# Layer 1 of a two-layer decoder trunk: the first group's scores are put three product steps earlier

## The chip, the cores and the metric

The kernel runs on one core of one Trainium2 chip. The metric is the device time of one execution in microseconds, as the median of several runs. The engines are named as in the profile: PE (TensorE matmul), PEld (its weight loads), DVE (VectorE), ACT (ScalarE), POOL (GpSimd), SP (SyncE, which issues the weight transfers). A code such as L439 is line 439 of the kernel before.

## The reference, cut to what matters

One sequence of 256 tokens, width 1024, two layers, 16 heads of 64. Layer 0 has an attention of its own with q, k and v. Layer 1 projects only q; its k and v have 4 heads and come from the residual stream in front of it. Each layer ends with a gated feed-forward with a causal convolution of width 3.

```python
hk = rmsnorm(x, kv_norm)
k, v = jnp.split(hk @ w_kv_b, 2, axis=-1)
shared_k = to_bhsd(partial_rope(heads(k, N_KV_HEADS), cos, sin))
shared_v = to_bhsd(heads(v, N_KV_HEADS))
...
h = rmsnorm(x, attn_norm[l])
q = partial_rope(heads(h @ w_q_b[i], N_HEADS), cos, sin)
o = swa_sink_attention(to_bhsd(q), shared_k, shared_v, sinks_b[i])   # window 128, a sink per head
x = x + o.transpose(0, 2, 1, 3).reshape(B_, S_, N_HEADS * HEAD_DIM) @ w_o
x = x + conv_ffn(rmsnorm(x, ffn_norm[l]), w_up[l], conv_w[l], conv_b[l], w_down[l])
```

## The kernel before, in words

All matrices are float32. Each operand of a large product is split into a high part (rounded to the matmul's format) and a low part (the rest), and a product is three matmuls: high by high, high by low, low by high. Weights come in units of 128 x 2048. SP transfers a unit (L170), ACT makes its high part (L181), DVE its low part (L189, or L191 with a gain), POOL the low part of a few (L187). Four units have room at a time.

The 256 tokens are two blocks of 128, b = 0 and 1. In layer 1, `q_half(a)` projects eight heads of q: for each block 8 steps of three products of 512 columns (L345 to L347, a "query step"), then `rotate`: ACT copies the result (L1013), DVE applies the rotary (L374 to L380, "the rope"), PE transposes (L386), ACT makes the high part of the transposes (L397) and DVE the low part (L392). The first half, `q_half(0)`, is run in full; the second is filler for the attention.

`attention` goes over four groups of four heads. `scores(g)` first issues six products of block 0 (L432 to L434), then twelve of block 1 (L439), which need the high and low parts of both blocks. Then the softmax: DVE adds the mask and takes the extreme (L457), ACT the exponential (L468), POOL merges (L463), DVE and ACT normalise (L473, L480, L478). `probs_T` transposes a pair of heads (L493), and ACT and DVE copy it out (L502, L499). `values(g)` is sixteen products with v (L538), copied out by ACT (L545, high) and DVE (L546, low). The filler after the second query half is the output projection, `Down.units(0, 3)`: units 0, 1 and 2 of it, each in four steps of six products (L587, L588, L590), called U1 to U12 in order of issue. Unit k needs the output of group k. Unit 3 and the additions to the residual (`finish`) come after the attention, and then the feed-forward (products L680 to L682).

The order of issue is written by a planner in the Python code. It has a clock of its own in nanoseconds that each piece of PE work advances by `tick`. Work for the other engines is put off with `chain(key, (wait, step), ...)`: a step is issued at the first tick at or past its due time, and the next step's wait counts from there. `require(key)` issues at once what is left under a key. A query step ticks 640 (L345 to L347), a step of the projection 1280. `fill(ns)` adds to a budget and takes filler steps until it is at or below zero; the rest is carried on:

```python
ready(oT)
fill(lead)
manual.close()
n_g = NH // 4
state = scores(0)
for g in range(n_g):
    pT = []
    for p in range(2):
        fill(rate(g)[p])
        pT.append(probs_T(2 * g + p, state[p]))
    fill(rate(g)[2])
    if g + 1 < n_g:
        state = scores(g + 1)
    ...
    values(g, pT)
```

From the attention of layer 0 on, the issued order is a priority: the program is scheduled so that an engine whose next instruction is not ready in the scheduler's reckoning takes a later one that is. On the chip each engine then runs its list in order.

Of the kernel before, what the change touches and what calls it, by code (L numbers as in the profile page):

```python
# [61 lines left out]
def trunk(ctx: ExitStack, tc, x, xw, pos, cpk, fin, w, out):  # L62
# [20 lines left out]
    def quad(dt=F32R, name="q"):  # L83
        return spaced(qd, 4 * S, dt, "q", nm(name), 15).rearrange("p (c t) -> p c t", c=4)
# [9 lines left out]
    def bank(tag):  # L94
        return ps.tile([P, 512], F32, tag=tag, name=nm(tag), bufs=4 if tag == "acc" else 2)
# [241 lines left out]
    def proj(o, hT, b, wv, units=()):  # L337

        n = o.shape[-1]
        o = pairs(o)  # L340
        for c in range(KC):
            require("x", b, c // 4)
            xh, xl = hx(hT, c)
            wh, wl = (turns(t) for t in wv(c))
            nc.tensor.matmul(o, xh[:, blk(b)], wh, start=(c == 0), stop=False)  # L345
            nc.tensor.matmul(o, xh[:, blk(b)], wl, start=False, stop=False)  # L346
            nc.tensor.matmul(o, xl[:, blk(b)], wh, start=False, stop=(c == KC - 1))  # L347
            tick(3 * n / 2.4)
            if units and (c + 1) * len(units) % KC == 0:
                used(units[(c + 1) * len(units) // KC - 1])  # L350
            yield 3 * n / 2.4

    def cols512(u):
        def wv(c):
            need(u + c // 4)
            hi, lo = wq[u + c // 4]
            s_ = slice((c % 4) * 512, (c % 4 + 1) * 512)
            return hi[:, s_], lo[:, s_]
        return wv
# [39 lines left out]
    def rotate(o, n, b, hi, lo, key, copy, then=None, wait=750.0, turn=1000.0):  # L399

        t = mid()[:, :n * P]
        chain(key, (150.0, lambda: copy(t)),
              (wait, lambda: rope(t.rearrange("p (h d) -> p h d", d=HD), 2 * n, b)),
              (turn, lambda: to_feature(t, n, b, hi, lo, key, then)))
# [499 lines left out]
    def diagonal(g):  # L904
        return lambda p: (kd[g % 2][:, p, 0], kd[g % 2][:, p, 1])

    mask = one.tile([P, S], F32, name="mask")
# [11 lines left out]
    qk = {}  # L919
# [89 lines left out]
    qk = {}  # L1009

    def q_out(t, b, o):
        require("rs", b)
        nc.scalar.activation(t, o, AF.Copy, scale=rs1[b])  # L1013

    def q_half(a):
        hi, lo = quad(), quad()
        u = U_QB + 2 * a
        for b in range(NB):
            o = bank("acc")
            yield from proj(o, xT, b, cols512(u), (u, u + 1) if b else ())  # L1020
            rotate(o, 4, b, hi, lo, ("qk", 2 * a), lambda t, b=b, o=o: q_out(t, b, o),
                   turn=2500.0 if a else 1000.0)
        for g in (2 * a, 2 * a + 1):
            c = slice(2 * (g % 2), 2 * (g % 2) + 2)
            qk[g] = (hi[:, c], lo[:, c], kT[:, 0:2], kT[:, 2:4], lambda p, a=a: a, lambda p, a=a: diagonal(0)(a))

    run(q_half(0))
    o_down = []

    def filler_b():  # L1030
        yield from q_half(1)
        yield from o_down[0].units(0, 3)
# [1 line left out]
    def ready_b(oT):  # L1034
        o_down.append(Down(U_OB, 4, oT, lambda i: require("o", i)))

    attention(qk, ready_b, filler_b(), 2800.0, lambda g: (2700.0, 1400.0, 1000.0) if g else (3300.0, 1700.0, 1000.0), mask, lambda h: 2 * (h // 8) + h % 2, True)

    hT = new_hT()
    y = [quad(F32, "y") for _ in range(2)]  # L1040
# [151 lines left out]
```

## Time and profile before

| | |
|---|---|
| median of 3 runs | 548.95 us (548.45 to 549.39) |
| the profiled execution | 548.46 us, span 546.7 us |
| busy, share of the span | PE 98%, weight loads 90%, DVE 76%, ACT 68%, POOL 24% |
| granted TensorE clock | 0.998 |
| the second query half to the feed-forward's first product | 311.24 to 364.78 us |
| first transposes of the half's last block, first scores L432, L439 | 314.48, 314.83, 316.54 us |

Times in a timeline are microseconds from the start of the span: start, length, engine, line, operation, output and inputs, shapes, and how many instructions of the kind follow each other; square brackets hold idle time of the engine in front of it and what ended that. The rows of PE overlap, since a product's end is modelled with its way through the array; the step from start to start is what it takes. In the table of waits stand who waited for whom, the sum in us, how often, and the longest.

### The profile page before, as it was taken

Reading aid. Unit: us, or ns where it says so; the run is one execution under the profiler, and the core shown is the slowest. Engines: PE = TensorE matmul, PEld = TensorE weight load, DVE = VectorE, ACT = ScalarE, POOL = GpSimd, SP = SyncE. Lnnn points to the kernel's source line nnn. Section 1 sums busy time; section 2 is a strip of 40 time slices with the busy share of each in tenths; the row PEclk is TensorE's granted clock in tenths of the full one; section 3 lists DMA queues with packets and bytes.
Section 4 is the critical chain, followed back from the end, with each engine's and each line's share of the span. In section 5 each row is a group of like instructions: output and inputs, shape, how many; then the busy total and the mean of one; then the engine's idle time right before and its main releaser. Section 6 shows DMA issues by size and latency. Waiting matters only on the chain.

```text
span 546.7 us, 9919 instructions
## 1 busy us (share of the span) xinstructions
PE 538.3 (98%) x3742; PEld 494.1 (90%) x3742; DVE 417.8 (76%) x869; ACT 372.7 (68%) x731; POOL 129.2 (24%) x164
## 2 busy tenths in 40 slices
PE   9999999999999999999999999999999999999995
PEld 7888888899999999988888887779999999998884
DVE  6798778689798888874467788798888888884414
ACT  6989776678568777744358689687657777764314
POOL 7322102012422333220001155102232322330003
PEclk9999999999999999999999999999999999999999
DMA  8974445342565665666553534232375556666201
GB/s 313 399 269 175 168 154 180 129 155 79 183 213 221 231 214 193 215 231 227 187 198 146 177 140 154 79 155 86 147 257 190 191 215 229 222 233 246 109 0 77
DMA packets 16464, 100.99 MB, mean 185 GB/s; under 512 B 1952, under 2 KB 2080, under 8 KB 5920
## 3 DMA queue, kind: packets, MB, share of 16 engines
q1 hardware_dynamic: 16128, 100.09, 51.2%
q8 instruction: 29, 0.48, 0.3%
q10 hardware_dynamic: 288, 0.26, 0.1%
q14 instruction: 19, 0.16, 0.1%
HBM read 99.30 MB, written 1.05 MB: 184 GB/s over the span
## 4 chain that ended last, share of the span: by engine, by line
PE 94%; ACT 3%; DVE 1%; DMA 1%; issue 0%; DVEq 0%; ACTq 0%
PE acc L587 9%; PE acc L588 9%; PE acc L590 9%; PE u L680 7%; PE u L681 7%; PE u L682 7%; PE t L680 6%; PE t L681 6%; PE t L682 6%; PE acc L345 5%; PE acc L346 5%; PE acc L347 5%; PE acc L792 2%; PE acc L680 2%; PE acc L682 2%; PE acc L681 2%
## 5 line engine op out<-in xcount | busy, mean ns | idle before, releaser
L189 DVE TENSOR_TENSOR wl<-wr,wh 128x1024 fp32r<-128x1024 f32 (+1 forms) x187 | 202.9, 1105 | 44.9 <-ACT wh L181 44.5
L181 ACT ACTIVATE wh<-wr 128x1024 fp32r<-128x1024 f32 (+1 forms) x190 | 176.2, 955 | 44.9 <-PE acc L590 39.5
L726 POOL TENSOR_TENSOR m<-m,m 128x256 f32<-128x256 f32 x44 | 70.7, 1606 | 168.6 <-DVE m L721 95.8
L587 PE MATMUL acc<-wh,q 128*128 128x512 f32 x238 | 92.1, 387 | 0.9 <-ACT q L545 0.8
L588 PE MATMUL acc<-wl,q 128*128 128x512 f32 x238 | 90.8, 382 | 0.0
L680 PE MATMUL u<-q,wh 128*128 128x256 f32 x320 | 88.3, 277 | 0.0
L681 PE MATMUL u<-q,wh 128*128 128x256 f32 x320 | 88.1, 276 | 0.0
L682 PE MATMUL u<-q,wl 128*128 128x256 f32 x320 | 88.0, 275 | 0.0
L681 PE MATMUL t<-q,wh 128*128 128x256 f32 x288 | 79.2, 275 | 0.0
L682 PE MATMUL t<-q,wl 128*128 128x256 f32 x288 | 79.2, 275 | 0.0
L680 PE MATMUL t<-q,wh 128*128 128x256 f32 x288 | 79.2, 275 | 0.0
L590 PE MATMUL acc<-wh,q 128*128 128x512 f32 x238 | 74.9, 381 | 0.0
L682 PEld LDWEIGHTS u<-q,wl 128*128 128x128 f32 x320 | 61.4, 192 | 0.0
L681 PEld LDWEIGHTS u<-q,wh 128*128 128x128 f32 x320 | 61.4, 192 | 0.0
L680 PEld LDWEIGHTS u<-q,wh 128*128 128x128 f32 x320 | 61.3, 192 | 0.2 <-DVE q L308 0.2
L680 PEld LDWEIGHTS t<-q,wh 128*128 128x128 f32 x288 | 55.3, 192 | 0.0
L681 PEld LDWEIGHTS t<-q,wh 128*128 128x128 f32 x288 | 55.3, 192 | 0.0
L682 PEld LDWEIGHTS t<-q,wl 128*128 128x128 f32 x288 | 55.3, 192 | 0.0
L730 ACT ACTIVATE q<-m 128x256 fp32r<-128x256 f32 x44 | 18.1, 416 | 50.5 <-POOL m L726 50.5
L587 PEld LDWEIGHTS acc<-wh,q 128*128 128x128 f32 x238 | 45.0, 189 | 8.0 <-ACT q L545 2.0
L590 PEld LDWEIGHTS acc<-wh,q 128*128 128x128 f32 x238 | 44.7, 189 | 6.5 <-DVE q L546 0.4
L588 PEld LDWEIGHTS acc<-wl,q 128*128 128x128 f32 x238 | 45.1, 190 | 5.8 <-issue 0.2
(182 smaller groups left out, 1039.1 us busy)
## 6 DMA issues: line engine op xcount, KB each, us to landing
wr<-in_w SPq DMA_DIRECT2D x82, 1024.0 KB, 4.8
wr<-in_w SPq DMA_DIRECT2D x16, 512.0 KB, 6.1
first<-in_xw SPq DMA_DIRECT2D x7, 384.0 KB, 6.2
xr<-in_x SPq DMA_DIRECT2D x2, 512.0 KB, 8.0
fin_t<-in_fin SPq DMA_DIRECT2D x1, 512.0 KB, 5.6
out<-ot SPq DMA_DIRECT2D x1, 512.0 KB, 2.6
first<-in_xw SPq DMA_DIRECT2D x1, 388.0 KB, 3.6
out<-m ACTq DMA_DIRECT2D x1, 256.0 KB, 2.1
```

The costliest lines, as they stand in the source:

```text
L181: nc.scalar.activation(wq[i][0][:, c], raws[i][:, c], AF.Copy, **({} if g is None else {"scale": g}))
L189: nc.vector.tensor_tensor(out=lo, in0=raw, in1=hi, op=ALU.subtract)
L345: nc.tensor.matmul(o, xh[:, blk(b)], wh, start=(c == 0), stop=False)
L346: nc.tensor.matmul(o, xh[:, blk(b)], wl, start=False, stop=False)
L347: nc.tensor.matmul(o, xl[:, blk(b)], wh, start=False, stop=(c == KC - 1))
L587: nc.tensor.matmul(o, ph[:, blk(b)], turns(hi[:, s_]), start=first, stop=False)
L588: nc.tensor.matmul(o, ph[:, blk(b)], turns(lo[:, s_]), start=False, stop=False)
L590: nc.tensor.matmul(o, pl[:, blk(b)], turns(hi[:, s_]), start=False, stop=end)
L680: nc.tensor.matmul(o, hi[:, s_], xh, start=(c == 0), stop=False)
L681: nc.tensor.matmul(o, hi[:, s_], xl, start=False, stop=False)
L682: nc.tensor.matmul(o, lo[:, s_], xh, start=False, stop=(c == KC - 1))
L726: nc.gpsimd.tensor_tensor(out=h, in0=gs, in1=t[1], op=ALU.mult)
```

## The change

Three numbers. For the second block of the first query half, the planner's wait from the copy to the rope goes from 750 to 550 and the one from the rope to the transposes from 1000 to 200. The lead, the filler issued in front of the first group's scores in layer 1, goes from 2800 to 900. The rates between the later events stay. The program has the same instructions.

```diff
             rotate(o, 4, b, hi, lo, ("qk", 2 * a), lambda t, b=b, o=o: q_out(t, b, o),
-                   turn=2500.0 if a else 1000.0)
+                   wait=750.0 if a or not b else 550.0, turn=2500.0 if a else 1000.0 if not b else 200.0)
...
-    attention(qk, ready_b, filler_b(), 2800.0, lambda g: (2700.0, 1400.0, 1000.0) if g else (3300.0, 1700.0, 1000.0), mask, lambda h: 2 * (h // 8) + h % 2, True)
+    attention(qk, ready_b, filler_b(), 900.0, lambda g: (2700.0, 1400.0, 1000.0) if g else (3300.0, 1700.0, 1000.0), mask, lambda h: 2 * (h // 8) + h % 2, True)
```

## The prediction

> **What bounds the kernel now.** I read the page first (busy time, the chain that ended last), then the table of stretches for the attention of layer 1, then PE's waits in it, then the timelines of PE, ACT, DVE and POOL there.
>
> ```profile
> span 546.7 us, 9919 instructions
> PE 538.3 (98%) x3742; PEld 494.1 (90%) x3742; DVE 417.8 (76%) x869; ACT 372.7 (68%) x731; POOL 129.2 (24%) x164
> ...
> PE 94%; ACT 3%; DVE 1%; DMA 1%; issue 0%; DVEq 0%; ACTq 0%
> ```
>
> ```profile
> 311.24:364.78 53.54, 52.47 (x338) 41.25 (x336) 44.52 (x151) 44.48 (x130) 16.64 (x30) 1.00 0.34 119
> ```
>
> ```profile
> PE acc L587 <- ACT q L545: 0.8, 1, 0.8
> ```
>
> PE is the bound: 98% of the span, 94% of the chain that ended last. The second fence is the stretch from the first product of the second query half (311.24) to the first product of the feed-forward (364.78): length, then busy time of PE, weight loads, DVE, ACT, POOL, then the granted clock (1.00). The change moves work inside this stretch and removes none, so it can only gain what PE idles there: by that row 53.54 - 52.47 = 1.07 us, nearly all of it one wait, the third fence. Busy time hides a little more, because a product's row (0.38) is longer than its step from start to start:
>
> ```profile
> 311.24 0.38 PE L345 MATMUL acc<-wh,q 128*128 128x512 f32 x1
> ...
> 314.26 0.38 PE L347 MATMUL acc<-wh,q 128*128 128x512 f32 x1
> ```
>
> These are the first and the last of 15 products (five steps of three): 3.02 us over 14 starts, 0.216 us each. Against that pace I find three waits later on:
>
> ```profile
> 325.55 0.48 PE L345 MATMUL acc<-wh,q 128*128 128x512 f32 x1
> 326.04 1.52 PE L538 MATMUL t<-pT,v 128*64 128x256 f32 x16
> ...
> 337.19 1.52 PE L538 MATMUL t<-pT,v 128*64 128x256 f32 x16
> 339.55 0.48 PE L587 MATMUL acc<-wh,q 128*128 128x512 f32 x1 [0.84 <-ACT q L545]
> ...
> 346.27 1.52 PE L538 MATMUL t<-pT,v 128*64 128x256 f32 x16
> 347.72 0.48 PE L587 MATMUL acc<-wh,q 128*128 128x512 f32 x1
> ...
> 348.69 0.59 PE L590 MATMUL acc<-wh,q 128*128 128x512 f32 x2
> 349.39 0.48 PE L587 MATMUL acc<-wh,q 128*128 128x512 f32 x1
> ```
>
> ```profile
> 338.92 0.57 ACT L545 ACTIVATE q<-t 128x512 fp32r<-128x512 f32 x1
> ...
> 348.76 0.57 ACT L545 ACTIVATE q<-t 128x512 fp32r<-128x512 f32 x1
> ```
>
> Sixteen value products take 1.45 us (346.27 to 347.72). So group 1's end at 338.64 and PE stands until 339.55: 0.91 us, until ACT has copied group 1's output (338.92 + 0.57 = 339.49). Two products from 348.69 end at 349.12, the next starts at 349.39: 0.27 us, behind ACT's copy of group 2 (ends 349.33). And 325.55 + 0.216 = 325.77 against 326.04: 0.27 us before group 0's values, some of it the change of shape. Together at most 0.91 + 0.27 + 0.27 = 1.45 us, 0.26% of the time.
>
> **The change part by part.** No instruction and no DMA is added or removed. Only the planner's numbers move.
>
> *Where things stand.* A query step ticks 640, a step of the output projection (a U step, six products) 1280; fill stops when its budget is at or below zero and carries the rest. Lead 2800 takes 5 query steps (rest -400), lead 900 takes 2 (rest -380). Carried on through the rates, the steps emitted ahead of each event are, before / after: scores of group 0: 5 / 2; scores of group 1: 14 / 11; scores of group 2: 16 and U3 / 16 and U2; scores of group 3: U7 / U6; last values: U11 / U10. Unit k of the projection (four U steps) needs the output of group k. So behind the values of a group there stand, free of that output: group 0: 2 query steps before, 5 after; group 1: one U step (U4) before, two after; group 2: one (U8) before, two after. Each U step is 6 x 0.216 = 1.30 us of cover.
>
> *The late waits.* In before U4 did not even stand behind group 1's values: PE took it ahead of group 2's scores, which waited for DVE's last transposed probabilities:
>
> ```profile
> 334.68 0.69 DVE L499 TENSOR_TENSOR pT<-t,v 128x512 f32<-128x512 f32 x1 [0.53 <-ACT pT L502]
> ```
>
> ```profile
> 334.84 0.59 PE L590 MATMUL acc<-wh,q 128*128 128x512 f32 x2
> 335.43 0.38 PE L432 MATMUL t<-kd,q 128*128 128x256 f32 x1
> ```
>
> The last two products of U4 start at 334.84, DVE is done at 335.37, the scores start at 335.43. The same wait can take one U step again; then the second still stands behind the values, and 1.30 covers 0.91. I take -0.91, and for group 2 -0.27 by the same count (1.30 more in front of 0.27). The bounds of both: 0, if both U steps are taken early, and these values. For group 0's values I take -0.15 (0 to -0.27): the three steps more stand in front of the same DVE multiplication.
>
> *The early side, where the cost is.* The second block's chain (copy, rope, transposes, high and low part) is unchanged in its work; its waits in the planner fall from 750 and 1000 to 550 and 200, and as the lead is two steps, `require` issues the transposes right after the rope.
>
> ```profile
> 311.44 0.69 ACT L1013 ACTIVATE m<-acc,rstd 128x512 f32<-128x512 f32 x1 [0.31 <-PE acc L347]
> 312.03 2.00 ACT L181 ACTIVATE wh<-wr 128x1024 fp32r<-128x1024 f32 x2
> 315.11 0.60 ACT L397 ACTIVATE q<-t 128x512 fp32r<-128x512 f32 x1 [1.08 <-PE t L386]
> ```
>
> ```profile
> 312.16 0.29 DVE L374 TENSOR_TENSOR rb<-m,cs 128x128 f32<-128x128 f32 x1
> ...
> 312.76 0.29 DVE L380 TENSOR_TENSOR m<-rb 128x128 f32<-128x128 f32 x1
> 313.12 2.36 DVE L189 TENSOR_TENSOR wl<-wr,wh 128x1024 fp32r<-128x1024 f32 x2
> 315.75 0.69 DVE L392 TENSOR_TENSOR q<-t,q 128x512 fp32r<-128x512 f32 x1 [0.27 <-ACT q L397]
> ```
>
> ```profile
> 314.48 0.60 PE L386 MATMUL t<-ident,m 128*128 128x128 f32 x4
> 314.83 0.36 PE L432 MATMUL acc<-kd,q 128*128 128x256 f32 x1
> ...
> 315.58 0.38 PE L345 MATMUL acc<-wh,q 128*128 128x512 f32 x1
> ...
> 316.23 0.38 PE L345 MATMUL acc<-wh,q 128*128 128x512 f32 x1
> 316.54 0.98 PE L439 MATMUL u<-q,q 64*128 64x256 f32 x12
> ```
>
> The copy cannot start before 311.44 and the rope ends at 313.05 at best. After six products PE stands at 311.24 + 6 x 0.216 = 312.54, so the transposes come 0.5 us too soon. From 313.1: transposes 0.35 and the first six score products 0.75 (314.48 to 315.58) bring PE to 314.2. The other twelve need the low part from DVE. The high part started 0.63 after the transposes (314.48 to 315.11), so it is due at 313.7, but ACT is at its two weight conversions until 314.03: it ends at 314.3 if the second is held back, else at 314.6. The low part takes 0.69; right behind the high part it ends at 315.0, behind DVE's two conversions (313.12 + 2.36 = 315.48) at 316.2. So these twelve start between 315.1 and 316.2, against 316.54 before, while nine products fewer stand in front of them (1.94 us). Filling nothing, PE would lose 1.94 - (316.54 - 316.2) = 1.6 us at worst, 1.94 - 1.44 = 0.5 at best. But in before PE put four products (315.58 to 316.23) into just this wait and lost 0.09. I take 0.3 for the places where the order is fixed too tightly; ends 0 and 1.6.
>
> *What is late next.* The second query half's last block has less in front of group 2's scores: 12 products instead of 18. Its chain costs what the first's does (0.69 + 0.9 + 0.35 + 0.6 + 0.6 = 3.1 us with the rope's 0.9 from 312.16 to 313.05); two U steps and a group of transposes cover 2.6 + 0.35, and a third U step is at hand. I take 0.2 for it, ends 0 and 0.9 (the cover of group 1's values, if it is used up here).
>
> *The queues.* SP issues the weights when conversions free their buffers, and their number and order stay. POOL is moved past: group 1's merges meet the four subtractions there, rival B.
>
> The sum: -0.91 - 0.27 - 0.15 + 0.3 + 0.2 = -0.83 us, from an execution of 548.46 (1.76 around its span) to 547.63. The median of the runs, 548.95, is 0.49 above that execution, so I predict 548.95 - 0.83 = 548.1.
>
> **The rivals.** A, nothing moves: the products are taken back into the early wait, and both U steps are gone before group 1's values. For it: U4 was taken early in before. Against it: the wait that took it was one U step long. 548.95 + 0.0.
>
> B, POOL holds group 1's softmax.
>
> ```profile
> 326.01 2.52 POOL L187 TENSOR_TENSOR wl<-wr,wh 128x512 fp32r<-128x512 f32 x2
> 328.50 0.87 POOL L463 TENSOR_TENSOR m<-m 128x128 f32<-128x128 f32 x2
> 329.54 0.46 POOL L463 TENSOR_TENSOR m<-m 128x128 f32<-128x128 f32 x1 [0.17 <-ACT m L468]
> 331.94 0.78 POOL L463 TENSOR_TENSOR m<-m 128x128 f32<-128x128 f32 x1 [1.94 <-ACT m L468]
> ```
>
> ```profile
> 331.19 1.22 DVE L189 TENSOR_TENSOR wl<-wr,wh 128x1024 fp32r<-128x1024 f32 x1
> ```
>
> Group 1's first merges follow POOL's subtractions without a gap, so exponentials that come 1.9 us sooner need not bring them sooner. Then the 0.91 stays: -0.27 - 0.15 + 0.5 = +0.1, 549.0. Against it: the last merge came at 331.94, released by ACT after 1.94 us in which POOL was idle. That merge took 0.78 instead of 0.46: it began under DVE's conversion and ended 0.35 after it. The Trainium skill ("SBUF — State Buffer", the summary of rules for kernel authors) says of VectorE with two SBUF inputs beside GpSimd that the second to issue fully blocks until the first is finished; this row agrees. By that rule each of the four merges could cost up to DVE's 1.22 more. By the rows a merge under a conversion costs 0.32 more, four of them 1.3 us, less than the 1.30 + 1.30 - 0.91 = 1.69 us that group 1's values have in hand, so the sum stays.
>
> C, slower: PE waits in a fixed order for the second block's low part, with nothing put in. 1.6 - 0.91 - 0.27 - 0.15 = +0.3 us; and if DVE puts one conversion of 1.18 ahead of the rope too, +1.4: 549.2 to 550.4. It decides from a wait of 1.33 us at the first group's scores. Against it: the four products put in there before.
>
> **How the numbers follow.** 0.2%, 1.1 us, is about what a measurement of this kernel can tell from no change. The forecast 0.70; its own range goes from all three waits gone at no cost (-1.45, 547.5) to a cost of 1.1 (-0.3, 548.65); 1.1 us of gain lies inside it, so 0.36 of it is faster, 0.34 within. A 0.10 and B 0.08, within. C 0.12, of which 0.03 within and 0.09 slower. Faster 0.36, same 0.55, slower 0.09. The range 547.4 to 549.4 leaves out the upper part of C and a small part below.
>
> **What would show it.** Right: no wait of PE for ACT's copy at group 1's values (0.84 before) and products at pace across group 2's; the transposes near 313.1, the first twelve-product scores between 315.1 and 316.2, and no wait above 0.3 us before them; the stretch to the feed-forward's first product 0.5 to 1.4 us shorter than 53.54. Wrong: a wait there of a microsecond (C), the 0.84 still there with merges right behind subtractions (B), or with U4 again ahead of group 2's scores and U3 too (A); or a change after 365, where nothing is moved.

## The result and the profile after

The changed kernel takes 555.39 us (median of four runs, 554.73 to 555.53) against 548.70 us before: ratio 1.0121, interval 1.0109 to 1.0133. It is 6.7 us slower, where 0.85 us of gain was forecast. The profiled execution took 555.53 us, its span 553.8.

The page of the kernel after, busy time and the chain that ended last:

```profile
PE 541.7 (98%) x3742; PEld 496.7 (90%) x3742; DVE 422.3 (76%) x869; ACT 372.2 (67%) x731; POOL 129.4 (23%) x164
...
PE 91%; ACT 3%; DVE 3%; issue 1%; POOL 0%; DVEq 0%; ACTq 0%; POOLq 0%
```

PE is "98% busy" in both, and the loss cannot be seen in that line. The chain shows it: PE's share went from 94% to 91%, DVE's from 1% to 3%, and "issue" (time in which an engine waited for nothing that the profile shows) from 0% to 1%. The stretch from the first product of the second query half to the first of the feed-forward, 53.54 us before, is now:

```profile
311.32:371.47 60.15, 55.40 (x338) 43.65 (x336) 49.14 (x150) 44.24 (x129) 16.00 (x30) 0.94 0.29 106
```

It is 6.61 us longer. PE idles 4.75 us in it instead of 1.07, and the same number of PE instructions is busy 2.93 us longer. The waits of PE over the whole span name the place:

```profile
PE t L386 <- DVE m L380: 2.6, 1, 2.6
...
PE acc L587 <- ACT m L1013: 1.0, 1, 1.0
```

The early side went as worked out, and the late waits are gone:

```profile
313.28 0.63 PE L386 MATMUL t<-ident,m 128*128 128x128 f32 x4 [0.17 <-ACT wh L181]
...
315.69 0.97 PE L439 MATMUL u<-q,q 64*128 64x256 f32 x12
...
334.66 0.59 PE L590 MATMUL acc<-wh,q 128*128 128x512 f32 x2
337.81 1.12 PE L386 MATMUL t<-ident,m 128*128 128x128 f32 x4 [2.55 <-DVE m L380]
338.57 0.78 PE L587 MATMUL acc<-wh,q 128*128 128x512 f32 x1
...
344.02 1.52 PE L538 MATMUL t<-pT,v 128*64 128x256 f32 x16
345.48 0.48 PE L587 MATMUL acc<-wh,q 128*128 128x512 f32 x1
```

The first group's transposes stand at 313.28 and its twelve-product scores at 315.69, where 313.1 and 315.1 to 316.2 were given. Behind group 1's values the next product follows in 1.46 us (344.02 to 345.48): the wait of 0.84 is gone. A new one of 0.26 us, for DVE's transposed probabilities, stands ahead of group 2's values (at 352.66). But in between PE stands still for the rope of the second query half's last block, and from there until 343.7 its products of 512 columns take 0.43 us from start to start instead of 0.216. The table of stretches has the reason, the granted clock (third number from the end):

```profile
336.00:338.00 2.00, 0.19 (x1) 0.19 (x2) 1.97 (x4) 0.24 (x1) 2.00 (x5) 0.71 0.36 66
338.00:340.00 2.00, 2.00 (x8) 1.73 (x8) 2.00 (x2) 0.60 (x1) 0.88 (x1) 0.50 0.95 401
340.00:342.00 2.00, 2.00 (x8) 1.73 (x7) 1.16 (x2) 0.00 (x0) 0.00 (x0) 0.50 0.41 115
342.00:344.00 2.00, 2.00 (x16) 1.67 (x15) 1.09 (x7) 0.70 (x4) 0.00 (x0) 0.58 1.02 430
```

What released the late transposes, followed back in order of time (start, length, work on the chain):

```profile
327.80 1.06 ACT wh L181
328.85 0.07 issue
328.92 0.47 POOL wl L187
329.39 0.66 issue
330.07 0.08 issue
330.15 1.28 POOL wl L187
331.43 0.42 POOL m L463
331.88 0.40 ACT m L478
332.28 0.27 ACT pT L502
332.55 0.95 ACT wh L181
333.49 0.59 ACT m L1013
334.11 0.89 DVE rb L374
335.00 1.36 DVE rb L379 x2
336.38 1.39 DVE m L380
337.76 0.04 issue
337.81 1.12 PE t L386 x4
```

A weight conversion on ACT releases two subtractions on POOL; group 1's last merge (L463) stands behind them in POOL's list; ACT, in order, waits 1.67 us for that merge before it normalises (L478), and only behind that, a copy and a further weight conversion does it copy the second half's last block (L1013), whose last product was done at 330.33. The rope then takes from 334.11 to 337.77, 3.6 us where it took 0.9.

Where does the conversion at 327.80 come from? It belongs to the next-to-last unit of the output projection, which has room once the twelfth query step, the 36th product of the second half, has read its unit; in the code that step also calls for the preparation of the unit four further on, which is this one. In before and after, that product and the conversion:

```profile
321.27 0.46 PE L347 MATMUL acc<-wh,q 128*128 128x512 f32 x1
```

```profile
322.28 1.05 ACT L181 ACTIVATE wh<-wr 128x1024 fp32r<-128x1024 f32 x1
```

```profile
326.45 0.38 PE L347 MATMUL acc<-wh,q 128*128 128x512 f32 x1
```

```profile
327.80 1.05 ACT L181 ACTIVATE wh<-wr 128x1024 fp32r<-128x1024 f32 x1
```

Group 1's scores stand after 14 query steps in before and after 11 in after. So the twelfth step fell behind them and behind group 0's values, and what hangs on it comes 5.5 us later, into group 1's softmax and the second half's last rope.

### The profile page after: what moved, and what is told of

Its sections match the earlier page's. It is cut to its first block, busy times and chain, and to the rows that moved or that the text cites. A ratio compares the mean times of both kernels' runs of the same rounds, so it can differ in the third digit from the quotient of the medians.

```text
span 553.8 us, 9924 instructions
## 1 busy us (share of the span) xinstructions
PE 541.7 (98%) x3742; PEld 496.7 (90%) x3742; DVE 422.3 (76%) x869; ACT 372.2 (67%) x731; POOL 129.4 (23%) x164
## 4 chain that ended last, share of the span: by engine, by line
PE 91%; ACT 3%; DVE 3%; issue 1%; POOL 0%; DVEq 0%; ACTq 0%; POOLq 0%
PE acc L587 8%; PE acc L588 8%; PE acc L590 8%; PE u L681 6%; PE u L682 6%; PE u L680 6%; PE t L682 6%; PE t L680 6%; PE t L681 6%; PE acc L345 5%; PE acc L346 5%; PE acc L347 5%; PE acc L792 2%; PE acc L682 2%; PE acc L681 2%; PE acc L680 2%
## 5 line engine op out<-in xcount | busy, mean ns | idle before, releaser
L189 DVE TENSOR_TENSOR wl<-wr,wh 128x1024 fp32r<-128x1024 f32 (+1 forms) x187 | 205.2, 1117 | 51.8 <-ACT wh L181 51.3
L587 PE MATMUL acc<-wh,q 128*128 128x512 f32 x238 | 93.0, 391 | 1.0 <-ACT m L1013 1.0
L590 PE MATMUL acc<-wh,q 128*128 128x512 f32 x238 | 75.0, 381 | 0.0
L345 PE MATMUL acc<-wh,q 128*128 128x512 f32 x128 | 50.1, 391 | 0.0
```

The source lines that it names most:

```text
L189: nc.vector.tensor_tensor(out=lo, in0=raw, in1=hi, op=ALU.subtract)
L587: nc.tensor.matmul(o, ph[:, blk(b)], turns(hi[:, s_]), start=first, stop=False)
L590: nc.tensor.matmul(o, pl[:, blk(b)], turns(hi[:, s_]), start=False, stop=end)
```

## The experiments

**Who subtracts.** All kernels are the changed kernel, or the one before as a control, with another choice of engine for the low parts of the last two projection units (in the code, unit U_OB + 2 and U_OB + 3):

```diff
-        if i == U_OB + 2 or i == U_OB + 3 and c.start:
+        if False:                                       # dve_sub, and before_dve_sub on the kernel before
+        if i == U_OB + 2 and not c.start:               # pool_first
+        if i in (U_OB + 2, U_OB + 3) and c.start:       # pool_last
+        if i == U_OB + 3:                               # pool_u3
```

> The changed kernel with all six subtractions of the last projection units on DVE instead of POOL. Theory 1 (POOL's subtractions hold back group 1's last merge, then stretch the rope of the second half's last block from 0.9 to 3.6 us; PE stands still and its clock halves): no wait of PE above 1 us from 328 to 345, granted clock 1.00 throughout, the rope's four instructions within 1.1 us, time 547.5 to 550. Theory 2 (the second half's last block simply comes too late in the order, whoever subtracts): PE still waits 1.5 us or more for that rope, time 552 or more.

> The kernel before with the same six subtractions on DVE: the control. Both theories: within 1.5 us of the kernel before (547.5 to 550.5), as POOL's subtractions there overlap no rope. If it gains as much as the changed kernel does, the subtractions on POOL cost the same in both, and theory 1 is wrong.

> The changed kernel with only the first two subtractions (of the unit that stands ahead of group 1's last merge) left on POOL, the other four on DVE. Theory 1, split: the merge still stands behind them and the copy of the second half's last block still comes at 333 or later, but the rope is not stretched (0.9 to 1.1 us), so PE's wait for it shrinks from 2.55 to under 1 us and the clock stays at 1.00; time 549 to 552. If the order of the merge alone were the cause: 553 or more.

> The changed kernel with the first two subtractions on DVE and the last four left on POOL. Theory 1, split: the last merge is free, the copy comes about 331, and the rope is through before POOL's first subtraction, so no wait over 1 us; time 548 to 551. If the rope still falls under a subtraction, it takes 2 us or more and the wait stays: 552 to 555.

> The changed kernel with POOL's subtractions moved one unit later: the next-to-last projection unit's on DVE, all four of the last unit on POOL. Theory 1: group 1's last merge is free and the rope is over before POOL subtracts (it takes 0.9 to 1.4 us), so no wait of PE over 1 us; 548 to 549.8, at or below the 549.8 with the last four subtractions on POOL. If the rope is again under a subtraction, 2 us or more for it and 550 or more.

| kernel | median, us | before, run beside it | ratio (95% interval) |
|---|---|---|---|
| changed, all on DVE (dve_sub) | 549.61 | 548.42 | 1.0023 (1.0014 to 1.0032) |
| before, all on DVE (before_dve_sub) | 550.43 | 548.42 | 1.0034 (1.0021 to 1.0047) |
| changed, first two on POOL (pool_first) | 551.96 | 548.42 | 1.0061 (1.0046 to 1.0076) |
| changed, last four on POOL (pool_last) | 549.82 | 548.42 | 1.0025 (1.0014 to 1.0035) |
| changed, last unit on POOL (pool_u3) | 549.03 | 548.37 | 1.0013 (1.0003 to 1.0022) |

Without POOL's subtractions the changed kernel is 1.2 us over before instead of 6.7; the kernel before gets 2.0 us worse by the same edit, where at most 1.5 was expected. So most of the loss is the subtractions' place. The changed kernel then stands 0.8 us below the control, but the two intervals overlap, and the gain is not where the sum had it. The wait for ACT's copy behind group 1's values, which was to vanish, in dve_sub and in the control:

```profile
PE acc L587 <- ACT q L545: 1.8, 1, 1.8
```

```profile
PE acc L587 <- ACT q L545: 0.7, 1, 0.7
```

In dve_sub all of U1 to U4 went ahead of group 1's values, so nothing was left to stand behind them: that is the mechanism of rival A. Its expectation of no wait above 1 us was wrong there. Its clock stayed at 1.00, and its rope's instructions take 0.28, 0.35 and 0.28 again, with a conversion of 1.22 among them. pool_first parts the two halves of the chain. The rope's rows in it, and POOL's in the kernel after beside the rope's there:

```profile
334.56 0.28 DVE L374 TENSOR_TENSOR rb<-m,cs 128x128 f32<-128x128 f32 x1
334.76 0.35 DVE L379 TENSOR_TENSOR rb<-m,sn 128x64 f32<-128x64 f32 x2
335.03 1.22 DVE L189 TENSOR_TENSOR wl<-wr,wh 128x1024 fp32r<-128x1024 f32 x1
336.17 0.28 DVE L380 TENSOR_TENSOR m<-rb 128x128 f32<-128x128 f32 x1
```

```profile
333.57 2.55 POOL L187 TENSOR_TENSOR wl<-wr,wh 128x512 fp32r<-128x512 f32 x2 [1.48 <-ACT wh L181]
336.07 0.32 POOL L451 COPY m<-nsink 128x2 f32<-128x2 f32 x2
336.35 2.54 POOL L187 TENSOR_TENSOR wl<-wr,wh 128x512 fp32r<-128x512 f32 x2
```

```profile
334.11 0.89 DVE L374 TENSOR_TENSOR rb<-m,cs 128x128 f32<-128x128 f32 x1 [0.83 <-ACT m L1013]
334.92 1.43 DVE L379 TENSOR_TENSOR rb<-m,sn 128x64 f32<-128x64 f32 x2
336.38 1.37 DVE L380 TENSOR_TENSOR m<-rb 128x128 f32<-128x128 f32 x1
337.68 2.29 DVE L189 TENSOR_TENSOR wl<-wr,wh 128x1024 fp32r<-128x1024 f32 x1
```

With the same merge behind the same two subtractions the copy is as late (333.28), but no subtraction runs under the rope: its instructions take 0.28, 0.35 and 0.28 again, the 2.6 us wait is gone, the clock stays at 1.00, and 3.2 us come back (6.7 over before became 3.5), though PE waits 1.76 us behind group 1's values here too. In the kernel after, each of DVE's rows, all with two operands in SBUF, waits for a subtraction (half of a row of two). The rope's end 0.13 to 0.23 us behind one: 335.00 behind 334.85, 336.35 behind 336.12, 337.75 behind 337.62. The conversion, 1.22 us when free, ends 1.08 behind the last one (339.97 behind 338.89). Freeing the merge too (dve_sub) gives 2.3 more. pool_last and pool_u3 fell between their two cases: one pair of instructions or one is still caught (the pair at L379 takes 1.43, L380 1.24), PE waits 0.9 us, and they cost 0.7 to 1.4 us over before.

**What of the change does it.** With the lead of 900 alone, and the two waits as before, the lists of all five engines come out the same as with all three numbers: the lead is the whole change. Two leads in between:

```diff
-    attention(qk, ready_b, filler_b(), 900.0, ...
+    attention(qk, ready_b, filler_b(), 1600.0, ...      # lead3: three query steps, group 1's scores after 12
+    attention(qk, ready_b, filler_b(), 2200.0, ...      # lead4: four, group 1's scores after 13
```

> The changed kernel with a lead of 1600: three query steps in front of the first group's scores. The twelfth query step is then the last one ahead of group 1's scores. Theory 1: as with four, 547.5 to 551, clock 1.00. Rival (the loss grows with the number of products moved): six of nine products moved, 552 to 554.

> The changed kernel with a lead of 2200: four query steps in front of group 1's... of the first group's scores instead of two (five before). The preparation of the next-to-last projection unit hangs on the twelfth query step; it then still stands ahead of group 1's scores (13 steps), as in before. Theory 1: no rope under a subtraction, no half clock, time 547.5 to 550.5, with at most a wait for group 1's merges behind four subtractions in a row. Rival (the loss grows with the number of products moved): three of nine products moved, 550.5 to 552.

548.27 (ratio 0.9995, 0.9986 to 1.0005) and 547.96 (0.9998, 0.9988 to 1.0007), against 548.37. The loss does not grow with the products moved: six of nine cost nothing, nine cost 6.7 us. It is a threshold, and it lies at the twelfth step: with twelve steps ahead of group 1's scores nothing is lost beyond the interval, with eleven 6.7 us.

**The threshold by itself.** The two halves of the same question: the first group's scores as in the change but the twelfth step ahead of group 1's, and the first group's scores as before but the twelfth step behind.

```diff
 after, step12_ahead:
-    ... 900.0, lambda g: (2700.0, 1400.0, 1000.0) if g else (3300.0, 1700.0, 1000.0), ...
+    ... 900.0, lambda g: (2700.0, 1400.0, 1000.0) if g else (3300.0, 1700.0, 1700.0), ...
 before, step12_behind:
-    ... 2800.0, lambda g: (2700.0, 1400.0, 1000.0) if g else (3300.0, 1700.0, 1000.0), ...
+    ... 2800.0, lambda g: (2700.0, 1400.0, 1000.0) if g else (2300.0, 1700.0, 100.0), ...
```

> The changed kernel with the third rate of group 0 raised from 1000 to 1700: the first group's scores stand just where the change puts them (two query steps ahead), but group 1's scores come after 12 query steps instead of 11. Theory 1, traced to its start (the conversion of the next-to-last projection unit waits for the buffer that the twelfth query step frees; behind group 1's scores that comes 5.5 us later, and with it POOL's subtractions): the loss is gone, 547.5 to 549.5, clock 1.00, the rope 0.9 us. Rival (it is the early scores of the first group that cost): 553 or more.

> The kernel before, lead 2800 and the first group's scores where they were (five steps ahead), but with the rates of group 0 cut to 2300, 1700, 100, so that group 1's scores come after 11 query steps as in the changed kernel. Theory 1, traced to its start: the loss appears without the change, 552 or more, a wait of PE for the second half's last rope over 1.5 us, and a granted clock of about half behind it. Rival (the early scores of the first group cost): 547.5 to 550.

548.54 us against 548.71 (ratio 0.9997, 0.9988 to 1.0006), and 552.92 (1.0071, 1.0051 to 1.0090). The first has the change's early scores and no loss; the second has the early scores of before and the loss's mark, the wait for the rope and the half clock:

```profile
336.70 1.12 PE L386 MATMUL t<-ident,m 128*128 128x128 f32 x4 [2.52 <-DVE m L380]
```

```profile
338.00:340.00 2.00, 2.00 (x6) 1.60 (x5) 2.00 (x3) 0.45 (x1) 0.00 (x0) 0.51 0.76 279
```

In step12_ahead the first four subtractions stand in a row ahead of group 1's merges and end 2.3 us before the rope:

```profile
324.04 5.00 POOL L187 TENSOR_TENSOR wl<-wr,wh 128x512 fp32r<-128x512 f32 x4 [1.79 <-ACT wh L181]
```

```profile
331.33 0.29 DVE L374 TENSOR_TENSOR rb<-m,cs 128x128 f32<-128x128 f32 x1 [0.96 <-ACT m L1013]
```

step12_ahead also shows what the late wait of the sum was worth, with the new loss kept out:

```profile
334.80 0.38 PE L432 MATMUL t<-kd,q 128*128 128x256 f32 x1 [0.58 <-DVE pT L499]
...
336.57 1.52 PE L538 MATMUL t<-pT,v 128*64 128x256 f32 x16
338.02 0.70 PE L590 MATMUL acc<-wh,q 128*128 128x512 f32 x2
```

The next product follows group 1's values in 1.45 us, so the wait behind them is gone. But PE now waits 0.58 us for DVE's last transposed probabilities ahead of group 2's scores, a wait that before filled with U4, and the time is 0.17 us under before, inside the interval.

step12_behind loses 4.2 us and not 6.7. Its wait for L1013 is absent (the 1.0 us of after), and its half clock lasts 3.4 us instead of 6.8; I did not part these further.

**The half clock.** Matmuls of a tile of ones are put where PE stood still, in the banks of the late transposes and of the coming scores, which overwrite them. The edits, in words:

```diff
 after, pe_kept_busy (to_feature, the second half's last block):
+        # eleven matmuls of ones x ones into pt, ahead of the four transposes
 after, pe_busy_twice: the same, and in scores(2):
+            # ten matmuls of ones x ones into sa, ahead of the first product
```

> The changed kernel with eleven matmuls of a tile of ones put in front of the late transposes of the second half's last block, into their own bank, which the transposes then overwrite: they fill the 2.7 us in which PE stands still for the rope and change no other order up to there. Theory 1c (2.8 us of the loss are the half clock that follows the standing still): the granted clock stays at 1.00 from 330 to 345, the transposes start at about the same time (337 to 338.2), time 552.0 to 553.5. Rival (the half clock has another cause, or costs nothing): 554.8 or more.

> The changed kernel with eleven matmuls of a tile of ones ahead of the late transposes and ten more behind them, into a bank of the coming scores, so that PE has work in both stretches in which it stood still when only the first was filled. Theory 1c (the half clock follows the standing still, and costs what PE does between DVE's end at 340.4 and 344): clock 1.00 from 334 to 346, no wait of PE over 0.5 us there, the time 1.0 to 2.3 us under that of the kernel with eleven alone (556.5), so 554.2 to 555.5. Rival (the half clock has another cause): it falls again at 337 to 344 and the time stays at 556 or more.

The first missed: 556.49 us (ratio 1.0140, 1.0123 to 1.0157), and the clock fell all the same. The matmuls filled the wait for the rope, but the order behind them changed, and PE then stood still for the last transposed probabilities on DVE, which stand in line behind a conversion of 2.29 us under a subtraction:

```profile
340.44 0.56 PE L432 MATMUL t<-kd,q 128*128 128x256 f32 x1 [2.15 <-DVE pT L499]
```

The second filled that too:

```profile
338.00:340.00 2.00, 1.99 (x18) 1.99 (x19) 2.00 (x1) 0.60 (x1) 1.08 (x1) 1.00 0.93 373
```

The clock stayed at 1.00, and 555.50 us came out (1.0118, 1.0103 to 1.0134), the upper end of what was expected: 1.0 less than with the first stretch filled alone, though the intervals overlap, and no less than the changed kernel. So standing still is what lowers the clock.

What the half clock costs, these totals do not say, because the ones took the place of work. In the changed kernel PE ran U3, six products of the projection, between the late transposes and group 2's scores (from 338.57, at half speed); here the ten matmuls (two rows each) stand there, and U3 comes later:

```profile
338.50 2.40 PE L428 MATMUL u<-ones 128*128 128x128 f32 x20
...
342.59 1.52 PE L538 MATMUL t<-pT,v 128*64 128x256 f32 x16
```

Group 1's values start at 342.59 instead of 344.02, and as the second half starts 0.21 us later in this execution, that is 1.6 us sooner. Six products at full speed, 1.30 us, would have had room in those 2.40. So an estimate from these rows is that the half clock is worth up to 1.6 us of the 6.7, and the chain through POOL, ACT and DVE the rest; no run shows the half clock's price by itself.

None of the kernels beats the one before beyond its interval.

## Why the prediction was wrong, by its own steps

*What bounds the kernel, where things stand, the early side.* Right. The counts of steps came out, products were put into the early wait (seven behind the first transposes), and PE waited 0.17 us for the first transposes.

*The late waits.* The count of U steps was right: in the changed kernel and in step12_ahead the wait behind group 1's values is gone. What that buys was not shown: step12_ahead has the change's early scores and none of the new loss, and gains 0.17 us, inside its interval, for -0.83 worked out, as a wait of 0.58 for DVE came in its place. lead3 and lead4, 0.10 and 0.41 under before, lie inside their intervals too. That dve_sub is 0.82 under its control is luck beside the -0.83, since the wait behind group 1's values is 1.76 there against 0.70, longer and not gone.

*The queues.* This step failed. "SP issues the weights when conversions free their buffers, and their number and order stay": they hang on query steps. These were counted against the scores under "Where things stand" (14 before, 11 after), but what the twelfth step releases was not, so a conversion and its subtractions on POOL that came 5.5 us later had a price of nothing. step12_ahead puts this one step back and the whole loss of 6.7 us is gone; step12_behind brings 4.2 us by it alone. Where the other 2.5 come from stays open.

*What is late next.* The right instruction, the second half's last block, and the wrong size: 0.2 us with 0.9 as the upper end, from the duration of its steps in a row. As waits of PE it measured 1.0 for the copy and 2.55 for the rope, and a half clock of 6.8 us came with them. Two things were left out: ACT's list, in which the copy came behind a normalisation that waited 1.67 us for POOL, and POOL's work under the rope, 3.6 us for 0.9.

*Rival A*, both U steps gone before group 1's values, did not come in the changed kernel. It came in dve_sub and pool_first, with a wait of 1.76 us each.

*Rival B* named the place (POOL ahead of group 1's merge) and gave it 0.08, but priced it as a gain that does not come (549.0). It asked what the merge would lose, and stopped there; the merge did lose, and ACT's list carried the loss to the copy. The sentence after it weighed the rule of blocked engines against merges, where it would not decide; where it did decide, DVE was the one blocked. The Trainium skill ("SBUF — State Buffer", the summary of rules for kernel authors) says that the second to issue fully blocks until the first is finished, and the rows above agree: the rope's end 0.13 to 0.23 us behind a subtraction. The merge that the prediction reads ended 0.31 us after the conversion by its two rows, not 0.35.

*Rival C* had a wait of PE in a fixed order, 549.2 to 550.4, at the first group's scores. The wait came at the third group's.

*The range.* A cost of 1.1 on -1.45 is -0.35, 548.6, where -0.3 and 548.65 stand; it decides nothing.

## What to carry to other kernels

When work is moved ahead of a step, list what that step releases: here a buffer, by it a conversion, by that a queue on an engine that no one looks at. Ask of each queue which instruction now stands behind which, and follow the one that waits into the next engine's list. A move that costs nothing for six products and 6.7 us for nine has crossed such a point; here two sizes in between found it.

## What the runs showed of the hardware

A DVE instruction with two operands in SBUF waits for the subtraction that runs on POOL: 0.29 became 0.89 and 1.37, two of together 0.35 became 1.43, a conversion of 1.22 became 2.29, while POOL's own, which had started first, stayed at 1.27 each (2.55 for two). It goes the other way too: in dve_sub a merge on POOL that began at 329.78, under a conversion on DVE (329.43 to 330.65), took 1.18 us instead of 0.46.

The granted clock went to one half in waits of PE of 2.55 us (the changed kernel) and 2.52 us (step12_behind), and at the end of one of 2.15 us (pe_kept_busy), and not in waits of 1.76 us (dve_sub and pool_first). The length of the wait alone does not decide it: in the changed kernel the clock fell between 336.8 and 337.0, about 1.6 us after the row of PE's last product had ended (335.25), with a wait of 1.03 us shortly before. It stayed at one half for 3.4 us in step12_behind and pe_kept_busy and for 6.8 us in the changed kernel, though PE was at work again. The Trainium skill ("TensorE: Matmul & The Clock Gate", why this matters for your kernels) advises no idle gaps over about 3 us; here gaps of 2.15 to 2.55 us were enough, and the measurement decides.
